# One core, a three-layer block in fp32: merged multiplies in the recurrence, and another order of its steps

## The chip, the cores and the metric

The kernel runs on one core of a Trainium2 chip. The metric is the time of one execution on the device, in microseconds; the median of several runs is compared.

## What is computed

Three layers follow each other on a sequence of 256 rows of 1024 numbers: attention with a feed-forward net, a gated recurrence (HGRN2) with a feed-forward net, and a mixed layer with a feed-forward net. Only the recurrence is touched:

```python
def hgrn2_mixer(x, lb, w_in, g_norm, w_o):
    h = x @ w_in
    q, f, i, g = jnp.split(h, [1024, 2048, 3072], axis=-1)
    q = jax.nn.silu(q)
    fg = lb + (1.0 - lb) * jax.nn.sigmoid(f)
    k = 1.0 - fg
    logf = jnp.log(fg)
    o = chunk_gated_linear(heads(q), heads(k), heads(i), heads(logf))
    o = rms_norm(o, g_norm) * jax.nn.silu(g)
    return o.reshape(B, T, D_MODEL) @ w_o

# S_t = diag(f_t) S_{t-1} + k_t v_t^T ; o_t = S_t^T q_t, 8 heads of 128 x 128
```

## The kernel before

The 256 rows are two tiles of 128 rows, numbered 0 and 1 (`t`). Every weight product is made of three matmuls, since a number is kept as a high and a low part (`rhi` and `rlo` of a weight, `xh` and `xl` of an activation): `mm3` at lines 226 to 228. One product of a tile with 512 columns of a 1024-row weight is 24 matmuls of 512 columns. The weight comes in four loads of 512 KB by the SyncE queue into `raw`; ScalarE makes `rhi` (line 175), VectorE makes `rlo` (line 177), or GpSimd does (line 182). There are nine buffers each of `rhi` and `rlo`, and the two parts of the log gates (`lfh`, `lfl`) of each tile live in the same buffers, one pair for each tile.

The method `hgrn` is the recurrence. It names its steps, and the string `HGRN` lists them in the order in which they are traced; a scheduler of the framework then puts each engine's instructions into one fixed order, each engine executing its own in that order. The steps are:

- `P.f0.0`, ..., `P.g1.1`: project tile 0 or 1 onto half of q, f, i or g (`project`, `evac`). The result goes to a bank of PSUM (`a`).
- `l.t`: logs of the gates of a tile; `t.t` (`turned`): transposes of q and k of a tile by TensorE (`t<-ident,q`, `t<-ident,f`), copied by ScalarE.
- `p.t.i` (`pair`): heads 2i and 2i+1 of tile t. Within a tile the sums over earlier rows are split in levels: seven, and an eighth for tile 1, which reads the state. TensorE makes the exponents of two levels at a time (`lx<-lev,lfh` and `lfl`, lines 876, 877), ScalarE takes exp into `e` (line 879), VectorE multiplies the late half of every block by q (line 886) and the early half by k (line 888, which for levels 2 and 5 is done by GpSimd). Then TensorE multiplies early with late halves: `lv<-e`, one 64 by 64 piece at level 0 (line 893), 64 by 32 pieces at levels 1 to 6 (line 899). These are small: they use 64 columns of the array. VectorE gathers them under masks in `blocks` (line 904), copies them to `attn` (line 240), and TensorE makes the output `o` of both heads (lines 915, 917). After every second pair the heads are normed (`norm_heads`, lines 318 to 322).
- `S` (`state`): the state that tile 0 leaves to tile 1 (two products with `suf` at lines 843, 844, exp at line 846, a multiply at line 847, products at line 850).
- `g.t.n` (`gated`): silu of g, two multiplies (VectorE line 937, GpSimd line 939) and transposes; `o.n.t`: output product; `n.t` closes a tile (layer norm), `z.0` turns tile 0 for the next stage.

In the order before, `p.0.0` and `p.0.1` stand together, then `t.1`, `P.i1.1` and `S`, then `p.0.2` and `p.0.3` after `P.g0.1`, and the pairs of tile 1 with `P.g0.0`, `P.g1.0` and `o.0.0` beside them.

Of the kernel before, what the change touches and what calls it, by code (L numbers as in the profile page):

```python
# [16 lines left out]
ALU = mybir.AluOpType  # L17
AX = mybir.AxisListType

P = 128  # L20
# [67 lines left out]
class Net:  # L88
# [701 lines left out]
    def hgrn(self, XT, dst):  # L790
        nc, ins = self.nc, self.ins
        w_in, w_o = ins["hgrn_w_in"][0], ins["hgrn_w_o"][0]
        lb, lev, msk, suf, id64, gn = self.hgrn_held
        fg, q, v, sg, qT, kT, lf, dg = ([None, None] for _ in range(8))

        def evac(kind, t, n, a):
            c = slice(n * 512, (n + 1) * 512)
# [25 lines left out]
        def turned(t):  # L823

            dg[t] = self.sm(t, 8, name="dg")
            qT[t], kT[t] = self.w4((P, 8, P), name="qT"), self.w4((P, 8, P), name="kT")
            for n in range(2):
                c, b = slice(n * 512, (n + 1) * 512), slice(4 * n, 4 * n + 4)
                qk = self.w2(t, (P, 4, P), name="qk")
                nc.gpsimd.tensor_tensor(qk.rearrange("p h d -> p (h d)"), q[t][:, c], fg[t][:, c], ALU.mult)  # L830
                nc.vector.tensor_reduce(dg[t][:, b], qk, AX.X, ALU.add)
                self.copy(qT[t][:, b, :], self.blocksT(self.cols(q[t], 4 * n, 4), "hT"), "h_qT")
                self.copy(kT[t][:, b, :], self.blocksT(self.cols(fg[t], 4 * n, 4), "hT"), "h_kT")

        S = [None]

# [19 lines left out]
        part = lambda y, l, s: y.rearrange("p j (b s e) -> p j b s e", s=2, e=64 >> l)[:, :, :, s, :]  # L856

        def pair(t, i):

            hs = slice(2 * i, 2 * i + 2)  # L860

            b = self.w1(i % 2, (P, 2, 64), name="blocks")
            w = self.w1(i % 2, (P, 2, P), name="attn")
            nc.gpsimd.memset(w[64:, :, :64], 0.0)
            eng = nc.gpsimd if "h_d" in ON_POOL else nc.vector
            eng.tensor_tensor(
                b, id64[:, None, :].to_broadcast([P, 2, 64]),
                dg[t][:, hs].rearrange("p (j o) -> p j o", o=1).to_broadcast([P, 2, 64]), ALU.mult,
            )
            for l0 in range(0, 7 + t, 2):  # L870
                m = min(2, 7 + t - l0)
                x = self.bank("hx%d" % (l0 // 2), (P, 2, 2, P), name="lx")
                rhs = lev[:, l0 * P : (l0 + m) * P].rearrange("p (l n) -> p l n", l=m)
                for j in range(2):
                    c = slice((2 * i + j) * P, (2 * i + j + 1) * P)
                    nc.tensor.matmul(x[:, j, :m, :], lf[t][0][:, c], rhs, start=True, stop=False)
                    nc.tensor.matmul(x[:, j, :m, :], lf[t][1][:, c], rhs, start=False, stop=True)
                e = self.w2(l0 // 2 % 2, (P, 2, 2, P), name="e")
                nc.scalar.activation(e[:, :, :m, :], x[:, :, :m, :], AF.Exp)
                for l in range(l0, l0 + m):  # L880
                    y = e[:, :, l - l0, :]
                    if l == 7:
                        nc.vector.tensor_mul(y, y, qT[t][:, hs, :])
                        continue

                    nc.vector.tensor_mul(part(y, l, 1), part(y, l, 1), part(qT[t][:, hs, :], l, 1))
                    eng = nc.gpsimd if "h_k%d" % l in ON_POOL else nc.vector
                    eng.tensor_tensor(part(y, l, 0), part(y, l, 0), part(kT[t][:, hs, :], l, 0), ALU.mult)
                lv = self.bank("hv%d" % (l0 // 2), (P, 2, 2, 64), name="lv")
                if l0 == 0:  # L890
                    for j in range(2):
                        y = e[:, j, 0, :]
                        nc.tensor.matmul(lv[:64, 0, j, :], y[:, :64], y[:, 64:], start=True, stop=True)
                for l in range(max(l0, 1), min(l0 + m, 7)):
                    for j in range(2):
                        for c in range(2):
                            y = e[:, j, l - l0, 64 * c : 64 * c + 64]
                            late = y.rearrange("p (b s e) -> p b s e", s=2, e=64 >> l)[:, :, 1, :]
                            nc.tensor.matmul(lv[64 * c : 64 * c + 64, l - l0, j, :32], y, late, start=True, stop=True)
                if l0 == 0:  # L900
                    self.copy(w[:64, :, 64:], lv[:64, 0, :, :], "h_w0")
                for l in range(max(l0, 1), min(l0 + m, 7)):
                    m3 = msk[:, l - 1, :].rearrange("p (b e) -> p b e", e=64 >> l)
                    nc.vector.copy_predicated(
                        part(b, l, 1), m3[:, None, :, :].to_broadcast([P, 2] + list(m3.shape[1:])),
                        lv[:, l - l0, :, :32].rearrange("p j (b e) -> p j b e", e=64 >> l),
                    )
            for c in range(2):
                self.copy(w[64 * c : 64 * c + 64, :, 64 * c : 64 * c + 64], b[64 * c : 64 * c + 64, :, :], "h_w%d" % (c + 1))
            if i % 2 == 0:  # L910
                self.ho = self.bank("ho", (P, 4, P), name="o")
            for j in range(2):
                h = 2 * i + j
                o = self.ho[:, h % 4, :]
                nc.tensor.matmul(o, w[:, j, :], v[t][:, h * P : (h + 1) * P], start=True, stop=t == 0)
                if t == 1:
                    nc.tensor.matmul(o, e[:, j, 1, :], S[0][:, h, :], start=False, stop=True)
            if i % 2:
                self.norm_heads(t, self.ho, 4, P, q[t][:, (i // 2) * 512 : (i // 2 + 1) * 512])
# [31 lines left out]
        def close(t):  # L951
            self.ln_residual(t, ys[t], *rows)

        self.run(
            HGRN, {"P": project, "l": logs, "t": turned, "p": pair, "S": state, "g": gated, "o": out, "n": close,
             "z": self.turner(dst)}
        )
# [358 lines left out]
WARM, WARM_X = 10, 13  # L1316
PIECE = 256
ON_POOL = {
    "b2_g0", "b2_kn", "b2_vm", "b2_w_out", "dsa_o", "h_d", "h_k2", "h_k5", "hgrn_f0", "hgrn_q1", "rk0b",
}  # L1320
ON_ACT = {
    "d_k", "d_kT", "d_relu0", "d_relu1", "d_s0", "d_s1", "d_up00", "d_up10", "d_up11", "d_v", "h_g", "h_kT", "h_lb",
# [42 lines left out]
)  # L1365
ASIDE = " x.0 x.1", " x.2"
HGRN = (
    "P.f0.0 P.f1.0 Z P.f0.1 P.q0.0 P.q0.1 P.f1.1 P.q1.0 P.q1.1 l.1 l.0 t.0 P.i0.1 P.i0.0 P.i1.0 p.0.0 p.0.1 t.1 P.i1.1 "
    "S P.g0.1 p.0.2 p.0.3 P.g0.0 p.1.0 p.1.1 g.0.0 p.1.2 p.1.3 P.g1.0 g.0.1 o.0.0 P.g1.1 g.1.0 o.1.0 g.1.1 o.0.1 n.0 "
    "z.0 o.1.1 n.1"  # L1370
)
MIX = (
# [79 lines left out]
```

## Time and profile before

| what | us |
|---|---|
| three runs: lowest, median, highest | 1143.95, 1149.02, 1149.86 |
| the profiled execution | 1149.55 |
| its span, first to last instruction | 1147.8 |
| TensorE matmul busy in the span | 1114.7 (97%) |
| VectorE, ScalarE, GpSimd busy | 686.3, 580.5, 204.4 |
| first `lx` of the recurrence to the first product of the next stage, by the timeline | 376.37 to 488.03 |

A busy TensorE is not TensorE at its peak: the ends of matmuls are modelled and overlap the next start, so what counts is from start to start. [...] The chain that ended last goes through TensorE for about a third of the span in its own steps, most of them the three lines of `mm3`.

### The profile page before, as it was taken

How to read it: one execution, taken by the hardware profiler on the slowest of the kernel's cores; microseconds unless marked ns; L12 is line 12 of the kernel's file. 1: busy time of each engine (PE TensorE's matmuls, PEld its weight loads, DVE VectorE, ACT ScalarE, POOL GpSimd, SP SyncE). 2: the span in 40 equal slices, each digit the busy share in tenths (PEclk: the TensorE clock that was granted, in tenths of full speed). 3: DMA queues.
4: the chain of work that ended last, by engine and by line, in shares of the span. 5: the costliest groups of instructions: out<-in, count | busy, mean ns of one | idle time of the engine just before them, and what ended most of it. 6: DMA issues, size and time to landing. Idle time of an engine off the chain costs nothing. (4 is left out here: it accounts for less than half of the span.)

```text
span 1147.8 us, 15285 instructions
## 1 busy us (share of the span) xinstructions
PE 1114.7 (97%) x5721; PEld 902.3 (79%) x5721; DVE 686.3 (60%) x1083; ACT 580.5 (51%) x828; POOL 204.4 (18%) x301
## 2 busy tenths in 40 slices
PE   8979999999999999999999999999999999999997
PEld 6546888888888777788888887887788878888886
DVE  6766745644656677975454586447646557554543
ACT  4475545544566456444453446663546455453441
POOL 2034440100431323100000011533100170000000
PEclk9989999999999899999999999999999999999999
DMA  8023656655545242465656454663454456566541
GB/s 293 21 90 92 206 199 220 222 172 184 159 144 189 94 142 78 135 216 175 230 166 204 149 167 148 209 154 110 161 183 147 147 157 217 176 221 202 169 143 37
DMA packets 98458, 187.33 MB, mean 163 GB/s; under 512 B 9400, under 2 KB 26952, under 8 KB 98384
## 3 DMA queue, kind: packets, MB, share of 16 engines
q1 hardware_dynamic: 94816, 176.28, 47.9%
q0 software_dynamic: 2864, 9.45, 2.6%
q8 instruction: 45, 0.74, 0.3%
q10 hardware_dynamic: 704, 0.62, 0.2%
q14 instruction: 29, 0.24, 0.1%
HBM read 185.28 MB, written 1.05 MB: 162 GB/s over the span
## 5 line engine op out<-in xcount | busy, mean ns | idle before, releaser
L177 DVE TENSOR_TENSOR rlo<-raw,rhi 128x1024 fp32r<-128x1024 f32 (+4 forms) x302 | 369.6, 1229 | 210.0 <-ACT rhi L175 197.8
L175 ACT ACTIVATE rhi<-raw 128x1024 fp32r<-128x1024 f32 (+4 forms) x334 | 347.9, 1047 | 230.1 <-PE y L228 79.6
L226 PE MATMUL a<-rhi,xh 128*128 128x512 f32 (+4 forms) x840 | 317.7, 379 | 2.5 <-ACT xh L175 1.1
L227 PE MATMUL a<-rlo,xh 128*128 128x512 f32 (+4 forms) x840 | 316.1, 376 | 0.5 <-DVE rlo L177 0.5
L228 PE MATMUL a<-rhi,xl 128*128 128x512 f32 (+4 forms) x840 | 314.7, 375 | 0.0
L226 PEld LDWEIGHTS a<-rhi,xh 128*128 128x128 f32 x840 | 158.3, 189 | 31.6 <-ACT xh L175 2.0
L227 PEld LDWEIGHTS a<-rlo,xh 128*128 128x128 f32 x840 | 158.5, 189 | 27.8 <-DVE rlo L177 1.0
L228 PEld LDWEIGHTS a<-rhi,xl 128*128 128x128 f32 x840 | 158.4, 189 | 27.3 <-DVE xl L177 0.2
L182 POOL TENSOR_TENSOR rlo<-raw,rhi 128x256 fp32r<-128x256 f32 x128 | 97.7, 798 | 206.1 <-ACT rhi L175 202.0
L226 PE MATMUL y<-rhi,hth 128*128 128x512 f32 x264 | 104.6, 396 | 0.5 <-ACT hth L175 0.5
L228 PE MATMUL y<-rhi,htl 128*128 128x512 f32 x264 | 103.1, 391 | 0.0
L227 PE MATMUL y<-rlo,hth 128*128 128x512 f32 x264 | 102.9, 390 | 0.0
L227 PE MATMUL y<-rlo,xh 128*128 128x512 f32 (+2 forms) x152 | 58.6, 385 | 1.8 <-DVE rlo L177 1.1
L226 PE MATMUL y<-rhi,xh 128*128 128x512 f32 (+2 forms) x152 | 58.7, 386 | 0.3 <-ACT rhi L175 0.3
L228 PE MATMUL y<-rhi,xl 128*128 128x512 f32 (+2 forms) x152 | 58.5, 386 | 0.0
L175 ACT ACTIVATE hth<-t 128x512 fp32r<-128x512 f32 (+1 forms) x36 | 20.1, 558 | 75.4 <-PE t L252 75.4
L226 PEld LDWEIGHTS y<-rhi,hth 128*128 128x128 f32 x264 | 49.6, 188 | 10.7 <-ACT hth L175 1.1
L228 PEld LDWEIGHTS y<-rhi,htl 128*128 128x128 f32 x264 | 49.6, 188 | 10.6 <-DVE htl L177 0.2
L227 PEld LDWEIGHTS y<-rlo,hth 128*128 128x128 f32 x264 | 49.6, 188 | 9.7
L700 DVE TENSOR_TENSOR sil<-a,sil 128x512 f32<-128x512 f32 (+1 forms) x36 | 23.2, 644 | 56.4 <-PE a L228 56.4
L694 ACT ACTIVATE sil<-a 128x512 f32<-128x512 f32 (+1 forms) x36 | 20.3, 563 | 66.0 <-PE a L228 65.9
L278 POOL TENSOR_TENSOR rs<-mv,nhalf 128x1 f32<-128x1 f32 x8 | 8.0, 996 | 241.8 <-DVE mv L283 241.8
(406 smaller groups left out, 1409.3 us busy)
## 6 DMA issues: line engine op xcount, KB each, us to landing
raw<-in_ffn_w_gate_dram SPq DMA_DIRECT2D x44, 512.0 KB, 4.7
raw<-in_ffn_w_up_dram SPq DMA_DIRECT2D x44, 512.0 KB, 4.7
raw<-in_ffn_w_down_dram SPq DMA_DIRECT2D x44, 512.0 KB, 4.5
raw<-in_hgrn_w_in_dram SPq DMA_DIRECT2D x32, 512.0 KB, 4.3
raw<-in_w_in_dram SPq DMA_DIRECT2D x24, 512.0 KB, 4.2
raw<-in_w_ffn_gate_dram SPq DMA_DIRECT2D x22, 512.0 KB, 4.7
raw<-in_w_ffn_up_dram SPq DMA_DIRECT2D x22, 512.0 KB, 4.8
raw<-in_w_ffn_down_dram SPq DMA_DIRECT2D x22, 512.0 KB, 4.5
```

The lines of the kernel that those rows point to most:

```text
L175: self.nc.scalar.activation(hi, src, AF.Copy)
L177: self.nc.vector.tensor_sub(lo, src, hi.bitcast(F32))
L182: eng.tensor_sub(lo[:, c], src[:, c], hi[:, c].bitcast(F32))
L226: mm(out, xh, wh, start=start, stop=False)
L227: mm(out, xh, wl, start=False, stop=False)
L228: mm(out, xl, wh, start=False, stop=stop)
L278: self.nc.gpsimd.tensor_tensor(r, v, self.nhalf[:, :n], ALU.pow)
L694: nc.scalar.activation(sil[ci, t][:, :cn], a[:, :cn], AF.Silu)
L700: nc.vector.tensor_mul(sil[ci, t][:, :cn], a[:, :cn], sil[ci, t][:, :cn])
```

## The change

Three things change, all within the recurrence. The transposed q and k no longer stand in two tiles for each t, but in one tile `QK` for each half of the heads. With both in one tile, each level's two multiplies (late half by q, early half by k) become one multiply of 128 by 256, whose operand `asked(l)` steps between the k and the q part; it is made by VectorE at every level, so the entries `h_k2` and `h_k5`, which sent a half to GpSimd, are gone. And the string `HGRN` has another order. The rest of the program is the same on every engine.

```diff
-        fg, q, v, sg, qT, kT, lf, dg = ([None, None] for _ in range(8))
+        fg, q, v, sg, lf, dg = ([None, None] for _ in range(6))
+
+        QK = {}
...
-            qT[t], kT[t] = self.w4((P, 8, P), name="qT"), self.w4((P, 8, P), name="kT")
             for n in range(2):
                 c, b = slice(n * 512, (n + 1) * 512), slice(4 * n, 4 * n + 4)
+                both = QK[t, n] = self.w4((P, 2, 4, P), name="QK")
...
-                self.copy(qT[t][:, b, :], self.blocksT(self.cols(q[t], 4 * n, 4), "hT"), "h_qT")
-                self.copy(kT[t][:, b, :], self.blocksT(self.cols(fg[t], 4 * n, 4), "hT"), "h_kT")
+                self.copy(both[:, 1, :, :], self.blocksT(self.cols(q[t], 4 * n, 4), "hT"), "h_qT")
+                self.copy(both[:, 0, :, :], self.blocksT(self.cols(fg[t], 4 * n, 4), "hT"), "h_kT")
...
-            hs = slice(2 * i, 2 * i + 2)
+            hs, n, j0 = slice(2 * i, 2 * i + 2), i // 2, 2 * (i % 2)
+
+            def asked(l):
+
+                x = QK[t, n][:, 0, j0 : j0 + 2, :]
+                w = 64 >> l
+                return bass.AP(tensor=x.tensor, offset=x.offset, ap=[x.ap[0], [P, 2], [2 * w, 64 // w], [4 * P + w, 2], [1, w]])
...
-                        nc.vector.tensor_mul(y, y, qT[t][:, hs, :])
+                        nc.vector.tensor_mul(y, y, QK[t, n][:, 1, j0 : j0 + 2, :])
                         continue
 
-                    nc.vector.tensor_mul(part(y, l, 1), part(y, l, 1), part(qT[t][:, hs, :], l, 1))
-                    eng = nc.gpsimd if "h_k%d" % l in ON_POOL else nc.vector
-                    eng.tensor_tensor(part(y, l, 0), part(y, l, 0), part(kT[t][:, hs, :], l, 0), ALU.mult)
+                    y = y.rearrange("p j (b s e) -> p j b s e", s=2, e=64 >> l)
+                    nc.vector.tensor_tensor(y, y, asked(l), ALU.mult)
...
 HGRN = (
-    "P.f0.0 P.f1.0 Z P.f0.1 P.q0.0 P.q0.1 P.f1.1 P.q1.0 P.q1.1 l.1 l.0 t.0 P.i0.1 P.i0.0 P.i1.0 p.0.0 p.0.1 t.1 P.i1.1 "
-    "S P.g0.1 p.0.2 p.0.3 P.g0.0 p.1.0 p.1.1 g.0.0 p.1.2 p.1.3 P.g1.0 g.0.1 o.0.0 P.g1.1 g.1.0 o.1.0 g.1.1 o.0.1 n.0 "
-    "z.0 o.1.1 n.1"
+    "P.f0.0 P.f1.0 Z P.f0.1 P.q0.0 P.q0.1 P.f1.1 P.q1.0 P.q1.1 l.1 l.0 t.0 P.i0.1 P.i0.0 P.i1.0 p.0.0 P.i1.1 p.0.1 "
+    "P.g0.0 t.1 p.0.2 P.g1.0 p.0.3 S g.0.0 p.1.0 P.g0.1 p.1.1 g.0.1 P.g1.1 p.1.2 o.0.0 p.1.3 g.1.0 o.1.0 g.1.1 n.0 "
+    "o.0.1 z.0 o.1.1 n.1"
 )
```

What this makes of the order on an engine is shown at three places. Lines are those of each kernel: 876, 877, 893, 899, 915, 843, 844, 850 before are 885, 886, 901, 907, 923, 845, 846, 852 now.

First, TensorE in pair `p.0.1`, of before (`t<-ident` are the transposes of `t.1`):

```order
L893 MATMUL lv<-e 64x64 x2
L877 MATMUL lx<-lev,lfl 128x128
L252 MATMUL t<-ident,q 128x128
L899 MATMUL lv<-e 64x32 x4
L252 MATMUL t<-ident,q 128x128
L915 MATMUL o<-i,attn 128x128 x2
L899 MATMUL lv<-e 64x32 x4
L252 MATMUL t<-ident,q 128x128 x2
L252 MATMUL t<-ident,f 128x128 x2
L899 MATMUL lv<-e 64x32 x4
L252 MATMUL t<-ident,f 128x128
L899 MATMUL lv<-e 64x32 x4
```

and of the change, from the same `lv` on:

```order
L901 MATMUL lv<-e 64x64 x2
L885 MATMUL lx<-lev,lfh 128x128
L907 MATMUL lv<-e 64x32 x8
L886 MATMUL lx<-lev,lfl 128x128
L907 MATMUL lv<-e 64x32 x4
L885 MATMUL lx<-lev,lfh 128x128
L886 MATMUL lx<-lev,lfl 128x128
L228 MATMUL a<-rhi,xl 128x512
L907 MATMUL lv<-e 64x32 x4
L226 MATMUL a<-rhi,xh 128x512
L907 MATMUL lv<-e 64x32 x4
L227 MATMUL a<-rlo,xh 128x512
```

The matmuls of 512 columns are those of `P.g0.0`; the transposes have moved behind the pair.

Second, TensorE at the state `S`, of before:

```order
L843 MATMUL a<-lfh,suf 128x512
L844 MATMUL a<-lfl,suf 128x512
L876 MATMUL lx<-lev,lfh 128x256
L877 MATMUL lx<-lev,lfl 128x256
L876 MATMUL lx<-lev,lfh 128x256
L226 MATMUL a<-rhi,xh 128x512
L227 MATMUL a<-rlo,xh 128x512
L228 MATMUL a<-rhi,xl 128x512
L850 MATMUL y_3620<-i,e 128x128 x4
```

and of the change:

```order
L923 MATMUL o<-i,attn 128x128 x2
L885 MATMUL lx<-lev,lfh 128x256
L886 MATMUL lx<-lev,lfl 128x256
L885 MATMUL lx<-lev,lfh 128x256
L886 MATMUL lx<-lev,lfl 128x256
L845 MATMUL a<-lfh,suf 128x512
L846 MATMUL a<-lfl,suf 128x512
L852 MATMUL y_3876<-i,e 128x128 x2
L226 MATMUL a<-rhi,xh 128x512
L852 MATMUL y_3876<-i,e 128x128 x2
L226 MATMUL a<-rhi,xh 128x512
L227 MATMUL a<-rlo,xh 128x512
```

Here `y` is the state's product. Six matmuls stood between it and the exponent `a` before; now it follows at once. The first `a<-rhi,xh` after it is the last quarter of `P.g1.0`, which the order has left until here.

Third, ScalarE at the same place in the change (`sq` is the square for the norm of `p.0.2` and `p.0.3`, the `rhi` behind it is that last quarter's weight):

```order
L175 ACTIVATE oh<-t 128x512
L888 ACTIVATE e<-lx 128x512
L318 ACTIVATE sq<-o 128x512
L848 ACTIVATE e<-a 128x512
L175 ACTIVATE rhi<-raw 128x1024
L848 ACTIVATE e<-a 128x512
```

The state's exp stands behind the square of the pair that ends just before it.

## Rows read from the trace of the kernel before

**Rows 1.** Windows, all engines: busy us (and instructions), granted clock, DMA share, GB/s
```profile
376.37:403.87 27.50, 26.12 (x200) 20.80 (x198) 18.95 (x53) 13.25 (x21) 10.66 (x14) 0.81 0.25 76
403.87:442.00 38.13, 37.02 (x327) 30.50 (x329) 28.80 (x88) 21.55 (x30) 9.48 (x17) 1.00 0.41 147
```

**Rows 2.** Windows of TensorE alone, the two at the ends of the half-clock stretch
```profile
387.00:388.00 1.00, 0.58 (x2) 0.66 0.00 0
397.00:398.00 1.00, 1.00 (x4) 0.72 0.00 0
```

**Rows 3.** Timeline of TensorE within the half-clock stretch, idle before it in brackets
```profile
387.42 1.22 PE L915 MATMUL o<-i,attn 128*128 128x128 f32 x4 [0.48 <-DVE attn L240]
388.80 0.64 PE L899 MATMUL lv<-e 128*64 128x32 f32 x8 [0.16 <-DVE e L886]
```

**Rows 4.** Waits of TensorE, 376 to 482 us: total, times, longest
```profile
PE o L915 <- DVE attn L240: 1.0, 2, 0.6
PE lv L893 <- DVE e L888: 0.6, 1, 0.6
PE a L226 <- DVE i L240: 0.5, 1, 0.5
PE lv L899 <- DVE e L888: 0.5, 2, 0.3
PE a L843 <- ACT e L846: 0.2, 1, 0.2
```

**Rows 5.** Timeline of TensorE at full clock: runs of small matmuls, and what follows
```profile
417.47 0.42 PE L899 MATMUL lv<-e 128*64 128x32 f32 x8
417.82 0.38 PE L876 MATMUL lx<-lev,lfh 128*128 128x256 f32 x1
418.14 0.43 PE L899 MATMUL lv<-e 128*64 128x32 f32 x8
...
441.82 1.36 PE L899 MATMUL lv<-e 128*64 128x32 f32 x40
443.11 0.39 PE L877 MATMUL lx<-lev,lfl 128*128 128x256 f32 x1
```

**Rows 6.** The level multiplies by source line: ns min, median, max, and first and last start
```profile
L886 DVE TENSOR_TENSOR e<-e,qT x56: 275/284/1259, 377.7 to 459.5; 128x128 f32<-128x128 f32 x56
L888 POOL TENSOR_TENSOR e<-e,kT x16: 447/507/1759, 378.2 to 457.2; 128x128 f32<-128x128 f32 x16
```

**Rows 7.** Timeline of VectorE: a multiply of a whole level, and the state's two multiplies
```profile
437.22 0.41 DVE L883 TENSOR_TENSOR e<-e,qT 128x256 f32<-128x256 f32 x1
...
403.74 1.29 DVE L847 TENSOR_TENSOR e<-e,f 128x512 f32<-128x512 f32 x2
```

**Rows 8.** Timelines of ScalarE, VectorE and GpSimd: last pair's norm and gate
```profile
465.94 0.60 ACT L318 ACTIVATE sq<-o 128x512 f32<-128x512 f32 x1 [5.28 <-DVE rlo L177]
...
466.95 0.68 DVE L320 TENSOR_REDUCE ss<-sq 128x4 f32<-128x512 f32 x1
469.99 0.69 DVE L322 TENSOR_TENSOR q<-o,rs 128x512 f32<-128x512 f32 x1 [0.56 <-POOL rs L278]
473.08 0.69 DVE L937 TENSOR_TENSOR q<-q,g 128x512 f32<-128x512 f32 x1
...
468.92 1.04 POOL L278 TENSOR_TENSOR rs<-ss,nhalf 128x4 f32<-128x4 f32 x1 [4.36 <-DVE ss L283]
473.85 1.29 POOL L939 TENSOR_TENSOR q<-q,gn 128x512 f32<-128x512 f32 x1 [3.89 <-DVE q L937]
```

**Rows 9.** Timeline of TensorE: last output of the recurrence, products, the last gate's transposes
```profile
465.47 0.39 PE L917 MATMUL o<-S,e 128*128 128x128 f32 x2
...
467.54 0.39 PE L226 MATMUL y<-rhi,oh 128*128 128x512 f32 x1
467.77 0.39 PE L227 MATMUL y<-rlo,oh 128*128 128x512 f32 x1
...
475.74 0.60 PE L252 MATMUL t<-ident,q 128*128 128x128 f32 x4
```

More of the change, by code (lines that the diff above doesn't have):

```diff
@@ L1318 @@
 ON_POOL = {
-    "b2_g0", "b2_kn", "b2_vm", "b2_w_out", "dsa_o", "h_d", "h_k2", "h_k5", "hgrn_f0", "hgrn_q1", "rk0b",
+    "b2_g0", "b2_kn", "b2_vm", "b2_w_out", "dsa_o", "h_d", "hgrn_f0", "hgrn_q1", "rk0b",
 }
```

## The prediction

> **What bounds the kernel now.** I took the windows first, with the clock's column, over the whole span; almost everywhere TensorE runs dense from start to start at full clock, and no edit of the recurrence's other engines could show there. The recurrence is another matter. In its first 27.5 us [rows 1] the mean clock is 0.81, in the 38.1 us behind it 1.00. The windows of one us [rows 2] show why: the window from 387 has 0.66, so the clock stays full for x of it with x + 0.5(1 - x) = 0.66, x = 0.32; the window from 397 has 0.72, half clock for 0.56 of it. [...]
>
> Then the waits of TensorE [rows 4]: 2.8 us in the recurrence, named for the copy to `attn`, the level multiplies, the copy of i and the state's exp. VectorE is busy 18.95 + 28.80 = 47.75 us of the 65.63 in the two windows [rows 1], so it is near, but not over, the limit. The third thing is what a run of small matmuls costs beyond itself. From one run of eight `lv` to the next, with one `lx` between, are 418.14 - 417.47 = 0.67 us [rows 5]. Forty `lv` in a row, up to the next `lx`, take 443.11 - 441.82 = 1.29 us, at most 0.032 each, so eight are 0.23 without the change of form at their ends; the `lx` alone is about 0.12, half the interval of a 512-column product, 467.77 - 467.54 = 0.23 [rows 9]. The rest, 0.67 - 0.23 - 0.12 = **0.32 us, is what each change to the small form and back costs.**
>
> **The change part by part.** The sum is made against the profiled execution, 1149.55 us, which is 0.53 above the median of the runs shown.
>
> *The half-clock stretch goes.* In the new order P.i1.1 stands beside p.0.0 and P.g0.0 beside p.0.1, and the transposes behind them, so the sparse stretch before 387 is filled. TensorE was idle 0.48 + 0.16 = 0.64 of the 10.24 us [rows 3]; the other 9.60 would take half at full clock. **-4.8 us.** The ends are 0, if the clock falls elsewhere, and -4.8.
>
> *The named waits.* The copies to `attn` (1.0), the level multiplies (0.6 and 0.5) and the copy of i (0.5) [rows 4] stood where TensorE had nothing else in its order; products stand there now. **-2.6 us**; the 0.2 before the state's exponent stays in the state's step below. The ends are 0 and -2.6.
>
> *The merged multiplies.* There were 56 by q on VectorE, median 0.284 us, and as many by k of the same size: 16 on GpSimd, median 0.507 [rows 6], the other 40 on VectorE. A multiply of a whole level takes 0.41 [rows 7]. So VectorE's part changes by 56 x 0.41 - 96 x 0.284 = -4.3 us of busy time at most, and GpSimd loses 8. I count **0** for it: what TensorE waits for is the end of a chain of matmul, exp and multiply, whose length changes by 0.1 us or so, and its cover is the products beside it. If that cover were gone, a level would end 0.16 us earlier than by two multiplies in a row on VectorE; where GpSimd had a part, that part alone took 0.45 to 1.76 [rows 6], 0.04 to 1.35 more than the whole level now. The block copy and its memset keep their places.
>
> *More changes of form.* Counted between the first `lx` and the last `lv` in TensorE's order, there are 39 runs of `lv` before and 47 now, since products are set between them. 8 x 0.32 = **+2.6 us**. The ends are 0, where a run is parted at a place where TensorE would have waited, and +2.6. [...]
>
> *The state's step.* S was traced early, with six matmuls between its exponent and its product; now it comes after p.0.3, and the product follows at once, as the second place in the order shows. ScalarE has the square of p.0.3's output ahead of the state's exp there. From the start of the last `o`: 0.47 until the square (465.94 against 465.47 [rows 8, 9]), 0.60 for it [rows 8], as much for the exp of the same size, 0.65 for a multiply (half of 1.29 [rows 7]): 2.3 us. TensorE has four `lx` of 0.12 and two products of 0.23 in that time, 0.94. So it stands about 1.4 us. Behind it the last quarter of P.g1.0 needs its `rlo` from VectorE, which has the norm ahead of it; that is covered by two products and four `lx` or not. I take **+1.5**, with ends 0 and +4 (the norm's chain of 0.68 + 1.04 + 0.69 us [rows 8] in full ahead of the `rlo`). This quarter is late because its weight can't be split earlier: two of nine `rhi` buffers hold logs, four hold g0 until P.g0.1, so three are left for g1, and the fourth frees up with S.
>
> *The end of the stage.* Before, 10.27 us lay between the start of the last `o` and the transposes of the last gate [rows 9], full of products. Now 19 products of 0.23 stand there, 4.4 us. The chain is 0.47 to the square, then 0.60, 0.68, 1.04, 0.69, 0.69 and 1.29 [rows 8], 5.5 us, with about 0.1 for each hand-over 6. **+1.5 us.** The ends are 0 and 5.8 (VectorE as full of weight splits as before). The layer norm of tile 0 comes later by as much and has its 18 products; I cost it at nothing.
>
> *Loads.* SyncE's queue has the same loads in the same order; the DMA share is 0.25 in the first window [rows 1]. Nothing.
>
> Sum: -4.8 - 2.6 + 2.6 + 1.5 + 1.5 = -1.8: 1147.75 by the profiled execution, 1147.2 by the median, and I say **1147.0 us**.
>
> **The rivals.**
>
> *A. The new waits are covered.* TensorE is slower by the additional changes of form, so chains end in time at S and at the end: 1149.55 - 4.8 - 2.6 + 2.6 = 1144.75, by the median 1144.2; with the eight runs parted where it would have waited anyway, 1141.6. For it: VectorE and GpSimd get 4.3 and 8 us back, and multiplies of up to 1.26 and 1.76 us [rows 6] stand where both worked at once. Against it: ScalarE's order at S.
>
> *B. The clock falls again, later.* Beside p.0.2 and p.0.3 the order has only 18 of P.g1.0's 24 matmuls, most before p.0.2's first `lv`; then p.0.2, p.0.3 and S follow with small matmuls and the 1.4 us wait, much as p.0.0 and p.0.1 did before 387. If TensorE's work there is as thin as ahead of 387, half clock comes back. The same 4.8 us at most: 1147.0 + 4.8 = 1151.8, **slower than before**; with the end's wait near 5.8 it is over 1155. It decides at S: a wait of much over 1.5 us brings it. [...]
>
> *C. A merged multiply is slow.* Its operand steps over runs of one to 64 numbers. If it took the 0.69 us of 512 columns [rows 8], 56 x 0.28 = 16 us more on VectorE, which has 18 us free in the two windows [rows 1]; a third of it on the path gives 1152. Against it: the halves have such runs as well and differ by little, 275 to 284 [rows 6].
>
> **How the numbers follow.** The forecast, 1144.5 to 1149.5, has 0.47; A 0.27, B 0.20, C 0.06. A range that holds eight in ten takes A's far end and B with one end of a wait: **1141 to 1153**. One can't tell a change of under 0.5% (5.75 us, the spread of the three runs) from none. Faster by more, under 1143.3, is the lower half of A and the far end of the forecast: 0.26. Slower by more, over 1154.8, is B or C with another wait at its end: 0.11. Within: 0.63.
>
> **What would show it.** Right: granted clock 1.00 from the first `lx` to the next stage; idle time before the state's product of 1 to 2 us, named for VectorE's `e`, and before the last gate's transposes, named for GpSimd's `q`; 56 multiplies of 128 by 256 at about 0.41; the stage's length, 111.66 us now by the timeline, about 110. Wrong: a clock of 0.50 in or after p.0.3 (B); no idle at S and at the end (A); multiplies over 0.5 (C); or a time that comes from a stage that the change doesn't touch.

## The result, and the profile after

The change made the kernel slower: 1153.39 us, the median of 11 runs (1150.13 to 1157.05), against 1146.73 us for the kernel before on the same chip (11 runs, 1142.34 to 1149.86). The ratio is **1.0068, 95% interval 1.0053 to 1.0084**. The forecast was 1147.0 us, within 1141 to 1153, and the range was just missed. Two single runs that took far longer, 3212.87 us in run 2 below and 2224.84 in run 5, are left out of the medians given there.

The profiled execution took 1153.68 us with a span of 1151.9, 4.1 over the profiled one of before. The recurrence, from its first `lx` to the first product of the next stage, took 117.32 us (373.89 to 491.21) instead of 111.66, so 5.7 more. Ahead of it 2.5 us less passed, behind it 0.9 more, though the order there is the same on every engine; in those parts two executions of one kernel differ nearly as much (the change began its stage 2.3 us earlier in run 11 below).

The same windows as in [rows 1], of the kernel after:

```profile
373.89:401.39 27.50, 26.02 (x193) 19.91 (x191) 17.89 (x41) 8.87 (x13) 4.02 (x6) 0.88 0.27 92
401.39:439.52 38.13, 36.33 (x314) 28.79 (x313) 25.90 (x66) 22.81 (x33) 8.60 (x13) 1.00 0.28 93
```

VectorE and GpSimd have less to do, as the diff says. But the mean clock of the first window, as a share of the full one, is 0.88, not 1.00. Windows of TensorE alone, one us each, with its clock third from the right, answer to [rows 2]:

```profile
390.00:391.00 1.00, 0.29 (x3) 0.89 0.00 0
391.00:392.00 1.00, 0.99 (x10) 0.50 0.00 0
397.00:398.00 1.00, 1.00 (x11) 0.69 0.00 0
```

By the working used for [rows 2], the clock is at 0.50 for 0.22 of the first and 0.62 of the last: from 390.78 to 397.62, for 6.8 us. In the window from 390, TensorE worked 0.29 us. The half-clock stretch is still there, 3.4 us shorter, still in `p.0.1`. Waits of TensorE in the stage, answering to [rows 4] (total, times, longest):

```profile
PE t L252 <- POOL q L947: 1.7, 1, 1.7
PE lv L907 <- DVE e L896: 1.4, 2, 0.7
PE lx L885 <- ACT e L888: 0.9, 2, 0.7
PE lx L885 <- DVE ol L177: 0.6, 1, 0.6
PE a L227 <- DVE rlo L177: 0.4, 1, 0.4
PE a L845 <- ACT e L848: 0.4, 1, 0.4
```

The old waits for `attn` and `i` are gone, and 5.4 us of waits stand there instead of 3.0 ([rows 4] has 2.8 and leaves out one wait of 0.2 for line 886). The second row is in `p.0.1`. TensorE's timeline there:

```profile
387.86 0.45 PE L901 MATMUL lv<-e 128*64 128x64 f32 x4
388.23 0.33 PE L885 MATMUL lx<-lev,lfh 128*128 128x128 f32 x1
388.49 0.42 PE L907 MATMUL lv<-e 128*64 128x32 f32 x8
389.60 0.42 PE L907 MATMUL lv<-e 128*64 128x32 f32 x8 [0.69 <-DVE e L896]
389.96 0.33 PE L886 MATMUL lx<-lev,lfl 128*128 128x128 f32 x1
391.01 0.64 PE L907 MATMUL lv<-e 128*64 128x32 f32 x8 [0.72 <-DVE e L896]
391.58 0.48 PE L885 MATMUL lx<-lev,lfh 128*128 128x128 f32 x1
391.85 0.42 PE L886 MATMUL lx<-lev,lfl 128*128 128x128 f32 x1
392.07 0.73 PE L228 MATMUL a<-rhi,xl 128*128 128x512 f32 x1
```

The products of `P.g0.0` that were to fill this place stand behind the `lv` that wait: the first of them starts at 392.07, when the clock has fallen. What the `lv` wait for is seen on VectorE and GpSimd:

```profile
387.38 3.58 DVE L896 TENSOR_TENSOR e<-e,QK 128x256 f32<-128x256 f32 x4
...
387.86 2.82 POOL L832 TENSOR_TENSOR qk<-q,f 128x512 f32<-128x512 f32 x2
```

Four level multiplies take 3.58 us while GpSimd makes the two `qk` multiplies of `t.1`. By the single records two of the four take 0.43 and 0.42 us, and two take 1.49 and 1.48, one over each `qk` (1.41 and 1.45). Elsewhere a merged multiply takes what was expected, as line 896 by itself shows (min, median, max in ns), to be set beside [rows 6]:

```profile
L896 DVE TENSOR_TENSOR e<-e,QK x56: 408/419/1491, 375.2 to 470.1; 128x256 f32<-128x256 f32 x56
```

At the end of the stage, answering to [rows 9]: 

```profile
474.72 0.39 PE L925 MATMUL o<-S,e 128*128 128x128 f32 x2
...
479.06 0.39 PE L226 MATMUL y<-rhi,oh 128*128 128x512 f32 x1
481.13 0.66 PE L252 MATMUL t<-ident,q 128*128 128x128 f32 x4 [1.68 <-POOL q L947]
```

Nineteen products end, and the transposes of the last gate come 1.7 us later, 6.4 us after the last `o`.

### The profile page after: what moved, and what is told of

The parts are those of the page before. It is cut to its first block, busy times and chain, and to the rows that moved or that the text cites. A ratio compares the mean times of both kernels' runs of the same rounds, so it can differ in the third digit from the quotient of the medians.

```text
span 1151.9 us, 15229 instructions
## 1 busy us (share of the span) xinstructions
PE 1117.1 (97%) x5721; PEld 901.0 (78%) x5721; DVE 680.1 (59%) x1043; ACT 583.1 (51%) x830; POOL 195.5 (17%) x285
```

## The experiments

The experiments are numbered, and "run 3" is the third. Two theories at first. **M**: the merged multiplies cost. **O**: the order costs. Later ones are named in the expectations. A ratio is to the kernel before on the same chip. "Excess" is a stretch's length less what its matmuls' columns take at full clock (an estimate by columns: a product 0.227 us, 256 columns of `lx` 0.12 and 128 half of it, an `lv` of 32 columns 0.027 and of 64 twice that, an `o` or a product of the state 0.11, a transpose 0.057; in sum some 85.6 us for the stage in every kernel). In dense stretches of the traces of before and of the change the starts lie 0.227 us apart for a product, 0.12 for `lx` of 256 columns and 0.11 of 128, 0.029 and 0.058 for `lv` of 32 and 64, 0.11 for `o` and the state, 0.109 for a transpose. By these the sum is some 3.8 us higher and every stage's excess as much lower; the differences between stages stay, those between pairs move with where the transposes stand, 0.05 us each. Each kernel's stage is shown by a row of its windows, with the columns of [rows 1]; its length is the second number, its mean clock the third from the right.

**1. The merged multiplies alone.** After, with the old `HGRN`:

```diff
-    ...P.i1.0 p.0.0 P.i1.1 p.0.1 P.g0.0 t.1 p.0.2 P.g1.0 p.0.3 S g.0.0 p.1.0 P.g0.1 p.1.1 g.0.1...
+    ...P.i1.0 p.0.0 p.0.1 t.1 P.i1.1 S P.g0.1 p.0.2 p.0.3 P.g0.0 p.1.0 p.1.1 g.0.0 p.1.2 p.1.3...
```

> The changed kernel with the old order of steps: the merged multiplies alone. TensorE's order has 45 runs of lv here (39 before, 47 in the change). If the new order is what costs (theory O), this stands at 0.998 to 1.002 of before. If the merged multiplies cost, by themselves or by the more finely parted lv runs that the scheduler makes of them (theory M: six more changes of form at 0.32 us, and a merged multiply that runs beside GpSimd's qk stretches as a whole), it stands at 1.002 to 1.005, 2 to 5 us over before. The forecast of the prediction, where the multiplies cost nothing, has 1.000 plus 1.9 us for the six changes of form, 1.0017.

```profile
374.50:482.74 108.24, 105.91 (x870) 85.18 (x868) 84.10 (x194) 58.93 (x82) 23.68 (x30) 1.00 0.35 111
```

1144.91 us, 0.9968 (0.9953 to 0.9982): faster than both kernels, clear of noise but small. No half clock in the stage of this execution. M falls; the result is even below the range that O gives.

**2. The new order alone.**

```diff
-                    y = y.rearrange("p j (b s e) -> p j b s e", s=2, e=64 >> l)
-                    nc.vector.tensor_tensor(y, y, asked(l), ALU.mult)
+                    qp, kp = QK[t, n][:, 1, j0 : j0 + 2, :], QK[t, n][:, 0, j0 : j0 + 2, :]
+                    nc.vector.tensor_mul(part(y, l, 1), part(y, l, 1), part(qp, l, 1))
+                    eng = nc.gpsimd if "h_k%d" % l in ON_POOL else nc.vector
+                    eng.tensor_tensor(part(y, l, 0), part(y, l, 0), part(kp, l, 0), ALU.mult)
```

The entries `h_k2` and `h_k5` are back in `ON_POOL` too; that line is not shown.

> The changed kernel with two multiplies for each level again, those by k of levels 2 and 5 on GpSimd: the new order alone. TensorE's order has 40 runs of lv. Theory O (the new order costs: the products set into the pairs of tile 1, S late, the end of the stage): 1.004 to 1.008 of before, as the change. Theory M (the multiplies cost): 0.998 to 1.002. The half-clock stretch stays in p.0.1 by both, since GpSimd's qk multiplies of t.1 still stand beside that pair's level multiplies.

```profile
376.25:498.09 121.84, 113.05 (x870) 89.65 (x868) 87.30 (x233) 61.08 (x84) 30.76 (x46) 0.93 0.30 99
```

1158.63 us, 1.0097 (1.0077 to 1.0118). O holds: the order alone costs 11 us, and the two parts multiply to 0.9968 x 1.0097 = 1.0065, about the change's 1.0068. The clock is at 0.50 in `p.0.1` for 6.8 us and, for 10.2 us, in `p.1.2` too.

It also corrects a count. TensorE's order has 45 runs of `lv` with the merged multiplies alone and 40 with the new order alone (39 before, 47 after). So most of the eight new runs come from the scheduler's answer to merged multiplies, not from products set between them.

**3. `qk` of `t.1` away from GpSimd**, in the change:

```diff
-                nc.gpsimd.tensor_tensor(qk.rearrange("p h d -> p (h d)"), q[t][:, c], fg[t][:, c], ALU.mult)
+                (nc.vector if t else nc.gpsimd).tensor_tensor(qk.rearrange("p h d -> p (h d)"), q[t][:, c], fg[t][:, c], ALU.mult)
```

> The changed kernel with the two qk multiplies of t.1 on VectorE (traced order puts them between the masked copies at the end of p.0.1) instead of GpSimd. Theory G (GpSimd's qk, 2.8 us, and the first four level multiplies of p.0.1 slow each other, which starves TensorE and lets its clock fall): the four multiplies take 1.4 to 1.7 us instead of 3.58, the waits of 0.69 and 0.72 us go, the clock stays at 1.00, and the time falls by 1.4 + 3.4 = 4.8 us against the change, to about 1.0025 of before. If the clock falls anyway because p.0.1 is thin in products, only the waits go: 1.4 us, 1.0055 of before. If neither: 1.0068, as the change.

VectorE's first four multiplies of `p.0.1` by its timeline, and the row of the stage:

```profile
391.04 1.43 DVE L896 TENSOR_TENSOR e<-e,QK 128x256 f32<-128x256 f32 x4
```

```profile
377.55:490.45 112.90, 108.36 (x869) 85.37 (x868) 82.76 (x195) 59.85 (x83) 18.84 (x28) 1.00 0.33 107
```

In this execution's stage all is as theory G has it: 1.43 us instead of 3.58, the waits of 0.69 and 0.72 us gone, the clock at 1.00 throughout, the stage 4.4 us shorter. The time is not: 1153.1 us, 1.0041 (1.0023 to 1.006). That interval touches the change's, and run 12 shows why.

**4. The same edit in the kernel before.**

> The kernel before with the two qk multiplies of t.1 on VectorE. The scheduler also moves the state's multiply ahead of the norm's on VectorE. Theory G: the copies to attn (1.78 us for two) and the first multiply of p.0.1 (1.26 us) go back to 0.45 and 0.28 us, the idle 0.48 and 0.16 us before the pair go, and if that was what let the clock fall, 10.24 us at half clock go as well, up to -5.1: 0.995 of before. If the clock falls anyway: 0.999 to 1.000.

```profile
374.86:482.08 107.22, 104.35 (x870) 84.81 (x869) 86.77 (x236) 59.20 (x82) 27.59 (x44) 1.00 0.33 110
```

1144.99 us, 0.9978 (0.9963 to 0.9994): a small gain, between the two expectations, and no half clock in this execution. Run 10 will show before's own stage without half clock at 108.05 us, so that 0.8 us is all that this edit takes off such a stage; that it keeps the clock up is not shown in the old order.

**5. Merged multiplies, old order, `qk` on VectorE** (edits 1 and 3).

> The merged multiplies with the old order (0.9968 of before by themselves) and the two qk multiplies of t.1 on VectorE. In the trace of the merged multiplies alone the clock stayed at 1.00 in the stage, and qk stretched three level multiplies to 2.25 us, about 1 us more than without it. If that 1 us is covered: 0.9968 again. If it is on the path: 0.996. If qk let the clock fall in some executions of the merged kernel after all: down to 0.993.

1143.60 us, 0.9991 (0.9966 to 1.0015), inconclusive (the two medians alone give 0.9973, within the interval). The stage took 108.18 us at 1.00, the same as run 1: the stretched multiplies were covered there.

**6 to 8. Moving products within the new order**, all with edit 3:

```diff
-p.1.2 o.0.0 p.1.3 g.1.0 o.1.0
+p.1.2 p.1.3 g.1.0 o.0.0 o.1.0
```

> The changed kernel with qk on VectorE (1.0041 of before), and o.0.0 in the order behind p.1.3 and g.1.0 instead of ahead of p.1.3: 24 more products between the last pair and the last gate's transposes. Theory E (the end's wait of 1.7 us for GpSimd's q is lost time, and products there get it back): the wait is gone, 1.5 us less and 1.0028; the lv runs fall from 47 to 44, which may give 1 us more, 1.002. Theory R (a product is needed in p.1.3 as much as at the end, and the wait only moves): 1.004, with new waits of TensorE in p.1.3 of 1 to 2 us.

```diff
-t.1 p.0.2 P.g1.0 p.0.3 S g.0.0
+t.1 S p.0.2 P.g1.0 p.0.3 g.0.0
```

> The changed kernel with qk on VectorE (1.0041 of before), and S back behind t.1, ahead of p.0.2, as in the old order. The rhi buffer of tile 0's logs is then not freed before p.0.3's exponents, but the state's product and its products of P.g1.0 are parted from p.0.3. Theory S (the late state, and the pairs p.0.2 and p.0.3 without a product beside them, cost): the excess of the stretch from p.0.2 to p.1.0, 10.9 us over what its columns take, falls by 2 to 3 us, 1.002. If the stretch costs as much in any arrangement: 1.004.

```diff
-S g.0.0 p.1.0 P.g0.1 p.1.1 g.0.1 P.g1.1 p.1.2 o.0.0 p.1.3 g.1.0 o.1.0 g.1.1 n.0 o.0.1 z.0
+S P.g0.1 p.1.0 p.1.1 g.0.0 p.1.2 p.1.3 g.0.1 o.0.0 P.g1.1 g.1.0 o.1.0 g.1.1 o.0.1 n.0 z.0
```

> The changed kernel with qk on VectorE (1.0041 of before), and from g.0.0 on the old sequence of steps (with P.g1.0 left at its new, early place). Theory T (the products set into the pairs of tile 1, and the end, cost): the excess in p.1.1 to p.1.3, 8.5 us, goes back to the 5.7 us of before, the end's 2.7 to 1.1 us, in all 4.3 us less: 1.0004. Theory S (the late state costs): 1.003 to 1.004.

1.0083 (1.0053 to 1.0112), 1.0104 (1.0074 to 1.0134) and 1.0067 (1.004 to 1.0094): none gained, all expectations of a gain missed. Their stages in order:

```profile
371.72:486.82 115.10, 109.94 (x869) 88.00 (x868) 83.50 (x196) 60.30 (x83) 18.98 (x28) 0.97 0.32 104
376.28:501.60 125.32, 116.45 (x870) 91.72 (x868) 83.67 (x195) 59.49 (x83) 17.83 (x28) 0.92 0.29 96
374.47:492.89 118.42, 112.22 (x870) 89.90 (x868) 84.26 (x196) 60.05 (x84) 19.14 (x28) 0.94 0.31 100
```

Run 6 shows how. Its end's excess fell from 2.7 to 0.95 us, as theory E had it; but `p.1.2` was left without a product, and a window of the stretch before and around its end reads:

```profile
454.00:460.00 6.00, 5.15 (x30) 4.49 (x31) 4.91 (x10) 2.53 (x4) 2.32 (x1) 0.50 0.30 87
```

Half clock. Run 7 has three such stretches (some 20 us together), run 8 two, which begin in `p.0.2` and in `p.1.2`:

```profile
408.00:416.00 8.00, 8.00 (x61) 6.46 (x60) 3.94 (x14) 1.63 (x4) 0.83 (x2) 0.57 0.00 1
459.00:467.00 8.00, 6.57 (x58) 5.70 (x58) 6.47 (x18) 2.25 (x5) 2.31 (x1) 0.57 0.23 67
```

The products are a fixed stock. Taken from one place, they are missing at another, and in runs 6 and 8 the clock fell in `p.1.2`, which had none. This is no rule: `p.0.3` in run 3 and `p.1.1` in run 9 have none either and kept the clock at 1.00, and run 7's stretches lie in pairs with 17 to 23 products, the first behind two waits of more than 1 us for ScalarE. The profiled executions were run 6's fastest (1149.50 us) and run 7's slowest (1164.53), so their stages show the kind of loss, not its mean.

**9. Old order for tile 0, new style for tile 1**, with edit 3; ahead of the first line all is old:

```diff
-p.1.0 p.1.1 g.0.0 p.1.2 p.1.3 P.g1.0 g.0.1 o.0.0 P.g1.1 g.1.0 o.1.0 g.1.1 o.0.1 n.0 z.0
+g.0.0 p.1.0 P.g1.0 p.1.1 g.0.1 P.g1.1 p.1.2 o.0.0 p.1.3 g.1.0 o.1.0 g.1.1 n.0 o.0.1 z.0
```

> Merged multiplies, qk on VectorE, the old order up to P.g0.0 (through the pairs of tile 0, with S early), and from p.1.0 on the new style: a product beside every pair of tile 1, and the new end. Theory T (the products beside the pairs of tile 1 and the thin end cost): the end's excess over its columns is 2.7 us instead of 1.1, the pairs p.1.1 to p.1.3 8.5 instead of 5.8, so 1.5 to 4.3 us more than the old order: 1.000 to 1.003 of before. Theory S (the head costs: S late, no product beside p.0.3): as the old order, 0.997 to 0.999.

```profile
373.87:488.90 115.03, 109.28 (x869) 86.76 (x868) 82.50 (x195) 61.50 (x85) 20.11 (x28) 0.99 0.35 109
```

Its longest wait of TensorE, at the end:

```profile
PE t L252 <- POOL q L947: 2.4, 2, 2.2
```

1151.41 us, 1.003 (1.0011 to 1.0048), the top of theory T's range and clear of S's. So tile 1 and the end cost without the new head, though the interval of run 5, with the old order throughout, reaches to 1.0015. The mean of 0.99 hides a half clock of 3.4 us at the end, from 479.0, just behind the wait of 2.2 us for `q`. Run 8 is the counterpart, the new head with the old sequence behind it: at 1.0067 against run 5's 0.9991 the head costs as well, in a profile with two falls.

**10 to 12. The same kernels again**, unchanged: before, after, and run 3.

> The kernel before, unchanged, in another execution. Theory F (the clock's fall depends on the execution as well as on the order): the stretch at 0.50 that began at 387.3 and took 10.24 us begins elsewhere, is shorter or is missing. If the order alone decides: 10.24 us again, at the same matmuls.

> The changed kernel, unchanged, in another execution. Theory F: the stretch at 0.50 that began in p.0.1, 16.9 us after the first lx, and took 6.83 us, is of another length, or a second one shows in p.0.2 to S. If the order alone decides: 6.83 us again at the same matmuls, and none else.

> The changed kernel with qk on VectorE again, in another execution. In the first its stage had no stretch at 0.50 and was 4.7 us longer than with the old order, while the medians lay some 8 us apart. Theory F: in other executions the clock falls in p.0.2 to S, as it did for 6.83 us in the kernel with the old sequence for tile 1, whose order on TensorE is the same up to there; this one shows such a stretch, or not, by chance. If the order alone decides: none, and a stage of 112.9 us again.

The stage of before, of another execution:

```profile
376.93:484.98 108.05, 104.46 (x870) 85.11 (x868) 87.83 (x234) 59.27 (x82) 31.79 (x46) 1.00 0.33 110
```

No half clock: 108.05 us instead of 111.66, with the same instructions in the same order. TensorE had idle time at the end of `p.0.0` and in `p.0.1` here too (its busy time is the first number behind the comma), and the clock stayed at 1.00:

```profile
386.00:388.00 2.00, 1.51 (x18) 1.04 (x16) 1.96 (x5) 0.42 (x2) 1.89 (x3) 1.00 0.00 1
388.00:390.00 2.00, 1.33 (x14) 1.13 (x15) 2.00 (x6) 0.00 (x0) 1.68 (x3) 1.00 0.00 0
```

The change had its fall in `p.0.1` again, at 389.2 for 6.8 us, and a stage of 117.54. Run 3's kernel, which had none, now had one in `p.0.2` and `p.0.3`:

```profile
408.00:412.00 4.00, 4.00 (x49) 3.28 (x48) 2.29 (x9) 0.98 (x2) 0.00 (x0) 0.80 0.00 2
412.00:416.00 4.00, 4.00 (x23) 3.27 (x23) 2.29 (x8) 1.19 (x2) 0.63 (x1) 0.50 0.00 0
416.00:420.00 4.00, 4.00 (x44) 3.12 (x43) 1.67 (x7) 0.98 (x2) 0.20 (x1) 0.85 0.01 2
```

and a stage of 115.82 us instead of 112.90. Theory F holds for two of the three kernels: with one order on TensorE, whether the clock falls in the stage differs between executions. Of five profiles of kernels with the old order one had a fall in the stage; of nine with the new order, or a good part of it, eight.

The fall in `p.0.1` is less a matter of chance in the new order. It came in all three profiles with `qk` on GpSimd (the change twice, run 2) and in none of the five with `qk` on VectorE (runs 3, 6, 7, 8 and 12). Four of these five have a fall later in the stage instead.

## Why the prediction was wrong, point by point

The table has, for each pair (up to the start of its first `o`) and for the end (from the last `o` on), the products of 512 columns in it and the excess in us. The first three columns had no half clock in the stage.

| | before, run 10 | merged alone, run 1 | new order with `qk` on VectorE, run 3 | after |
|---|---|---|---|---|
| p.0.0 | 9, 3.6 | 9, 3.6 | 26, 2.8 | 26, 2.8 |
| p.0.1 | 7, 3.2 | 9, 2.2 | 15, 2.3 | 17, 6.7 |
| p.0.2 | 50, 3.7 | 44, 4.2 | 25, 4.0 | 23, 4.0 |
| p.0.3 | 15, 1.6 | 19, 1.4 | 0, 3.2 | 0, 3.2 |
| p.1.0 | 14, 3.3 | 14, 4.2 | 32, 3.7 | 32, 3.7 |
| p.1.1 | 7, 1.5 | 7, 1.2 | 22, 2.8 | 22, 2.8 |
| p.1.2 | 11, 2.3 | 12, 2.8 | 18, 3.1 | 18, 3.1 |
| p.1.3 | 13, 2.1 | 17, 1.8 | 21, 2.7 | 21, 2.7 |
| end | 1.1 | 1.1 | 2.7 | 2.7 |
| stage | 108.05 | 108.24 | 112.90 | 117.32 |

**The step that failed first is "The half-clock stretch goes, -4.8".** In the profiled execution it was still there for 6.8 us, and the 3.4 us by which it was shorter are worth 1.7 by the prediction's own working, not 4.8. It failed twice. First, its base: the 10.24 us, from 387.32 to 397.56 by the two windows of [rows 2], belong to one execution. In the other profile of before they are missing, so 3.6 us of the 4.8 are not a property of the kernel that a better order could always get back. Second, the change did not fill the stretch. The prediction's own first place in the order has it: the first product of `P.g0.0` stands behind the `lv` of several levels, which wait for VectorE. The products behind the waiting `lv` covered nothing of their 0.69 and 0.72 us: the first started at 392.07. And the wait there grew: 1.4 us in `p.0.1`, where it was 0.7 in run 10, since four merged multiplies beside GpSimd's `qk` took 3.58 us. Run 3 took that cause away and 4.4 us of stage with it.

That multiplies take longer while GpSimd and VectorE both work stood in [rows 6], where they reach 1259 and 1759 ns against medians of 284 and 507; in the trace of before the first, from 387.40, stands beside GpSimd's two `qk` (386.01 to 388.50), the second, from 381.07, beside a `rlo` of 1.21 us on VectorE. The prediction used it only for the halves that GpSimd would no longer do, and overlooked that the `qk` remained on GpSimd, at the same time as the first multiplies of `p.0.1`. In the trace of the change the two long multiplies, 1.49 and 1.48 us, each end just behind one `qk` (1.41 and 1.45); in run 3, without `qk` on GpSimd there, the four took 1.43 us in all. By what means the engines hold each other up, no run shows.

**The named waits, -2.6**: wrong too. Those for `attn` and the copy of i went, but 5.4 us stand in the stage now: 1.4 in `p.0.1`, 1.7 at the end, 2.3 for exp, splits and the state. The 1.7 at the end and 0.8 at the state have terms of their own in the sum; the other 2.9 us are as much as before, so this term is about 0.

**The merged multiplies, 0**: right for stages without half clock, 108.24 us with them and 108.05 before, from one execution each. The gain of run 1 by the medians, 0.9968, is about the 3.6 us of a fall in `p.0.1`, whose excess is 2.2 us there instead of 3.2 without and 6.9 with a fall. That would need the fall in most executions of before, and one of its two profiles has none; that merging makes the fall rarer is not shown.

**More changes of form, +2.6**: about right, though not by its cause. Run 1 has six runs more; its named waits are 1.3 us shorter (2.2 against 3.5) and its stage as long, so six cost about 1.5 us, 0.25 each, if nothing else makes up for the waits. The prediction had 0.32; with the 0.032 that it gives as the most for one `lv`, eight are 0.26 and not 0.23, and the rest is 0.29. So 0.25 to 0.32 us is the estimate from these runs; what TensorE does in that time was not shown.

**The state's step, +1.5**: of the right size, but elsewhere. The state's product waited next to nothing; 0.4 us stand before its exponent and 0.4 before the `rlo` of the last quarter of `P.g1.0`. More is lost in `p.0.3`, just ahead of them, which has no product at all: 3.2 us of excess instead of 1.6, of which 0.6 is a wait of `lx` for VectorE's `ol`.

**The end of the stage, +1.5**: right, 2.7 against 1.1 us of excess, with a wait of 1.68 named for GpSimd's `q`.

**What the sum left out** is the pairs of tile 1. There were no idle times to fill in `p.1.1` to `p.1.3` beyond one of 0.6 us, for `attn` [rows 4], and with 61 products beside them instead of 31 they have 8.6 us of excess instead of 5.9. A part is runs parted further (18 against 13, some 1.3 us at 0.25). The named waits there are 0.9 us, in `p.1.2` and `p.1.3` for ScalarE's exp, instead of 0.6. The rest, about 1 us, no row names.

From run 10 to run 3 the stage grows by 4.9 us: 0.5 by named waits (4.0 against 3.5), 2.0 to 2.6 by eight runs at 0.25 to 0.32, and some 2 that neither accounts for. From run 3 to the change it is 4.4: 1.4 of waits in `p.0.1`, the rest half clock. Together 9.3 us between executions of which one had the fall and the other not; the medians, where before has it at times, differ by 6.7. How often each kernel has it, and what the 2 us are, stays open.

**The rivals.** B, "the clock falls again, later", at 1151.8 and with the end's wait over 1155, is what came nearest. Its place was wrong for the change, where the clock fell in `p.0.1`; in runs 8 and 12, in which `p.0.1` holds, it fell about where B said, at `p.0.2` and `p.0.3`, without S having to wait 1.5 us (1.1 us at its exponent in run 8, 0.4 in run 12); that limit was the author's estimate, and no run shows one. One order gave two outcomes, 111.66 us and, in run 10, 108.05, or 112.90 in run 3 and 115.82 in run 12; what decides between them was not shown. The fall should have been held for uncertain in the kernel before as well: then -4.8 is not certain, and the forecast is near no gain with the fall as a loss. A needed the clock at 1.00 and was wrong for that. C was wrong, 419 ns at the median.

## What to carry to other kernels

Ask whether work that is to cover a wait stands ahead of the waiting instruction in that engine's order: the products of `P.g0.0`, behind the waiting `lv`, covered nothing of 0.69 and 0.72 us. Where TensorE shows no idle time there is nothing to cover, while products set between small matmuls can add changes between kinds of matmul, 0.25 to 0.32 us each by the estimate above: `p.1.1` to `p.1.3`, with 30 products more, had 8.6 us of excess instead of 5.9. Products are a stock: ask of every place from which one is taken what is left there; in runs 6 and 8 the pair left without one lost the clock (0.50 and 0.57 in the windows above). Before a stretch at half clock is counted as a gain, look at a second execution of the same kernel: here it was 10.24 us in one and none in the other. And split a change that has two parts before keeping it: the merged multiplies under the old order, 0.9968, beat both kernels, though by little, and with `qk` moved as well (0.9991) the gain is not clear of noise.

## What was not expected of the hardware

The same instructions in the same order gave a stage of 111.66 or 108.05 us, by a stretch of 10.24 us at a clock of 0.50 that came or didn't; with the new order and `qk` on VectorE 112.90 or 115.82. Such falls also lie outside the stage: by windows of one us, 10.24 us at 0.50 from about 60 us on in the profiles of both before and the change, 3.4 us from 104 on in that of before alone and 3.4 from 258 on in that of the change alone, where both have the same order; a spread of 7.5 us in the runs of before is of that size. And two 1.4 us multiplies on GpSimd stretched four VectorE multiplies from 1.43 to 3.58 us, more than the price of making `qk` on VectorE itself (0.68 us each).
